# Two plain gate/up units instead of three at the edge into a feed-forward stage, with the third one's first two products as filler and a fixed order on three engines

## The chip, the core and the metric

The kernel runs on one core of one Trainium2 chip, in one launch. Times are device microseconds (us). The engines are TensorE (PE: matmuls and transposes, with its weight loads as PEld), VectorE (DVE), ScalarE (ACT), GpSimd (POOL) and SyncE (SP), which issues nearly all DMAs. Each engine takes its instructions in the order in which they stand in its own queue. Results of matmuls lie in PSUM, in eight banks; all else lies in SBUF.

## The reference

Two layers over a sequence of 512 tokens with 1024 channels. Layer 0 mixes tokens by stick-breaking attention, layer 1 by a gated MLP over chunks. Behind each mixer comes a SwiGLU feed-forward of width 2816, and this is where the change is:

```python
def swiglu(h, w_gate, w_up, w_down):
    return (jax.nn.silu(h @ w_gate) * (h @ w_up)) @ w_down

# at the end of a mixer, and ahead of the feed-forward behind it
x = x + gate * rms_norm(y, mix_post_g[i])
shift, scale, gate = ada_modulation(c, ffn_ada_w[i], ffn_ada_b[i])
h = rms_norm(x, ffn_pre_g[i]) * (1.0 + scale) + shift
y = swiglu(h, ffn_w_gate[i], ffn_w_up[i], ffn_w_down[i])
x = x + gate * rms_norm(y, ffn_post_g[i])
```

All is float32. The kernel multiplies in a shorter matmul type and makes up for it: each operand is split into a high part (ACT copies it to that type) and a low part (DVE subtracts the high part), and each product is three matmuls: high x high, high x low, low x high.

## The kernel before

The 512 tokens are four tiles of 128. `out_proj` (L545) ends a mixer: it accumulates the projection y of each tile in two PSUM banks, and hands each finished tile to `boundary` (L473). This makes, in order: the squares of y (ACT), their root, y times the gate G (DVE), the new residual x (DVE), its store (a POOL DMA), the squares of x and their root (ACT), the scaled and shifted t (DVE), eight transposes of t (PE) and the split of the transposed halves into hTh (ACT) and hTl (DVE). For tiles 0 and 1 it also keeps a float32 copy c (ACT). "Third tile" and "fourth tile" below are the tiles with tt of 2 and 3.

The feed-forward (`Ffn`, L1102) works on 22 pieces of 128 of its width. A plain unit (`unit`) makes gate and up of one piece for 256 tokens, as 2 x 8 x 3 matmuls of 256 columns; the first half takes tiles 0 and 1, the second half tiles 2 and 3. All other pieces go through `seven`, which makes gate and up for all 512 tokens together by seven products of half size, each 4 x 3 matmuls of 256 columns, instead of eight. For that it needs sums of the activations (`sums`: S1 to S4, from the kept copies c and the transposed third and fourth tile, split into Sh and Sl) and of the weights (`blocks`: x, b21, t13 and t24, each split; f13 and f24 are the float32 sums). A block's products stand in this order on PE: A11·B11 in bank R1, A12·B21 in R2, the previous block's A22·T4, then S1·T1 in a new bank R3, S2·T2 on top of R1, S4·B22 on top of R3, S3·T3 on top of R1. ACT copies R1 and R3 (tile e) before the next product is put on top. The generator `ahead` prepares the next block's weights in five steps between the products.

NH = 3: pieces 0, 1 and 2 are plain units, 3 to 21 are blocks. At the edge, `out_proj` takes the first halves of the three units (`first`, passed as `nxt`) one by one around the boundaries of the third and fourth tile; then come their second halves, then the blocks. Down to the second block the framework's scheduler decides where each engine's instructions stand. From there on (L1200) `pe["chain"]`, `dve.chain` and `act.chain` tie each instruction of the three engines to the one written before it.

Weights come by DMA on SP's queue, 512 KB each, into two `wraw` buffers (plain weights, and a block's x) and two `wraw2` buffers (a block's y). Their splits go to six pairs wh, wl. PSUM has six banks under tag b and two under tag p.

Of the kernel before, what the change touches and what calls it, by code (L numbers as in the profile page):

```python
# [8 lines left out]
F32 = mybir.dt.float32  # L9
F32R = mybir.dt.float32r  # L10
# [21 lines left out]
def trunk(ctx: ExitStack, tc: tile.TileContext, A: dict, out: bass.AP):  # L32
# [119 lines left out]
    def wemit():  # L152
# [4 lines left out]
        if src is None:  # L157
            for _ in blocks(*next_raws(n)):
                pass
            return  # L160
# [11 lines left out]
        else:  # L172
            act.activation(h[:], raw[:], AF.Copy)
            last_low[0] = nc.vector.tensor_tensor(l[:], raw[:], h[:].bitcast(F32), ALU.subtract)  # L174
# [31 lines left out]
    def blocks(xr, yr):  # L206

        fp = fwork["pool"]

        def high(t, src):  # L210
            act.activation(t[0][:], src, AF.Copy)

        def low(t, src):
            dve.tensor_tensor(t[1][:], src, t[0][:].bitcast(F32), ALU.subtract)

        def half(t, i):
            return lambda k: (t[0][:, 4 * i + k, :], t[1][:, 4 * i + k, :])

        x = wtile(KD, P)
        high(x, xr[:])  # L220
        f13 = fp.tile([P, KD, P], F32, tag="f13", name=nm("f13"))
        dve.tensor_tensor(
            f13[:].rearrange("p (a k) f -> p a (k f)", a=2),
            xr[:].rearrange("p (a k) f -> p a (k f)", a=2),
            yr[:, 4:8, :].rearrange("p (a k) f -> p a (k f)", a=1).to_broadcast([P, 2, 512]),
            ALU.add,
        )
        yield
        b21 = [fp.tile([P, 4, P], F32R, tag=f"b21{i}", name=nm("b21")) for i in range(2)]
        high(b21, yr[:, 0:4, :])  # L230
        t13 = wtile(KD, P)
        high(t13, f13[:])
        f24 = fp.tile([P, KD, P], F32, tag="f24", bufs=1, name=nm("f24"))
        dve.tensor_tensor(f24[:, 0:4, :], f13[:, 0:4, :], xr[:, 4:8, :], ALU.add)
        dve.tensor_tensor(f24[:, 4:8, :], f24[:, 0:4, :], yr[:, 0:4, :], ALU.add)
        yield
        low(x, xr[:])
        low(b21, yr[:, 0:4, :])
        yield
        t24 = wtile(KD, P)  # L240
        high(t24, f24[:])
        low(t13, f13[:])
        yield
        low(t24, f24[:])
        got.append({
            "B11": half(x, 0), "B22": half(x, 1), "B21": half(b21, 0),
            "T1": half(t13, 0), "T3": half(t13, 1), "T2": half(t24, 0), "T4": half(t24, 1),
        })

# [1381 lines left out]
```

## Time and profile before

| | us |
|---|---|
| median of 3 runs | 1125.38 |
| lowest, highest | 1118.23, 1127.74 |
| the profiled execution, its span | 1123.01, 1121.2 |
| edge of layer 0: first gate/up matmul, first matmul of a block | 276.6, 312.0 |
| edge of layer 1: first gate/up matmul | 772.2 |

The profile is of one execution. A row of the timeline gives start, length, engine, line in the kernel, operation, written tile <- read tiles and count; in brackets stands the idle time ahead of it and the instruction that ended it. Matmuls overlap: a row's length is that from its start to the modelled end of its result, and the distance to the next start is what it costs. An idle engine that nobody waits for costs nothing.

### The profile page before, as it was taken

How to read it: one execution, taken by the hardware profiler on the slowest of the kernel's cores; microseconds unless marked ns; L12 is line 12 of the kernel's file. 1: busy time of each engine (PE TensorE's matmuls, PEld its weight loads, DVE VectorE, ACT ScalarE, POOL GpSimd, SP SyncE). 2: the span in 40 equal slices, each digit the busy share in tenths (PEclk: the TensorE clock that was granted, in tenths of full speed). 3: DMA queues.
4: the chain of work that ended last, by engine and by line, in shares of the span. 5: the costliest groups of instructions: out<-in, count | busy, mean ns of one | idle time of the engine just before them, and what ended most of it. 6: DMA issues, size and time to landing. Idle time of an engine off the chain costs nothing.

```text
span 1121.2 us, 18515 instructions
## 1 busy us (share of the span) xinstructions
PE 1099.8 (98%) x7404; PEld 994.3 (89%) x7404; DVE 946.2 (84%) x1248; ACT 593.8 (53%) x982; POOL 29.6 (3%) x53
## 2 busy tenths in 40 slices
PE   6999999999999999999999999999999999999997
PEld 4787878788999999998888889988999999999995
DVE  4988999958989999879776867769979999899996
ACT  6454665656655555553253636437455555565652
POOL 0110100000000000000000000001000000000000
PEclk9999999999999999999999999999999999999999
DMA  8876434214424343359756375334224442332243
GB/s 335 331 246 208 148 91 131 91 59 155 161 78 167 132 162 121 114 208 345 251 192 243 132 269 164 101 125 150 96 95 151 149 147 89 106 113 95 76 142 122
DMA packets 51355, 176.38 MB, mean 157 GB/s; under 512 B 6074, under 2 KB 9146, under 8 KB 51268
## 3 DMA queue, kind: packets, MB, share of 16 engines
q1 hardware_dynamic: 48708, 166.81, 43.3%
q0 software_dynamic: 2560, 8.39, 2.1%
q8 instruction: 58, 0.95, 0.3%
q14 instruction: 29, 0.24, 0.1%
HBM read 164.69 MB, written 8.39 MB: 154 GB/s over the span
## 4 chain that ended last, share of the span: by engine, by line
PE 83%; DVE 9%; ACT 3%; DMA 3%; issue 2%; SPq 0%; DVEq 0%; ACTq 0%
PE r L107 33%; PE y L107 17%; PE v L107 8%; PE pqk L107 7%; PE u L107 4%; PE gu L107 4%; PE av L107 2%; PE z L107 2%; PE tw L115 1%; DVE wl L69 1%; DVE al L69 1%; DVE f L69 1%; DMA raw<-in_wdn 1%; DVE wl L174 1%; PE tp L115 1%
## 5 line engine op out<-in xcount | busy, mean ns | idle before, releaser
L85 ACT ACTIVATE wh<-raw 128x1024 fp32r<-128x1024 f32 (+1 forms) x112 | 115.7, 1037 | 134.5 <-PE y L107 44.1
L107 PE MATMUL r<-Sh,wl 128*128 128x256 f32 x608 | 170.2, 280 | 0.0
L107 PE MATMUL r<-Sh,wh 128*128 128x256 f32 x608 | 169.8, 279 | 0.0
L107 PE MATMUL r<-Sl,wh 128*128 128x256 f32 x608 | 169.6, 279 | 0.0
L107 PE MATMUL y<-wh,as 128*128 128x512 f32 x480 | 150.0, 390 | 0.0
L174 DVE TENSOR_TENSOR wl<-raw,wh 128x1024 fp32r<-128x1024 f32 x87 | 105.8, 1221 | 49.9 <-ACT wh L85 47.2
L107 PEld LDWEIGHTS r<-Sl,wh 128*128 128x128 f32 x608 | 114.3, 188 | 0.1
L107 PEld LDWEIGHTS r<-Sh,wl 128*128 128x128 f32 x608 | 114.1, 188 | 0.0
L107 PEld LDWEIGHTS r<-Sh,wh 128*128 128x128 f32 x608 | 113.7, 187 | 0.1
L107 PEld LDWEIGHTS y<-wh,as 128*128 128x128 f32 x480 | 90.0, 188 | 18.5
L69 DVE TENSOR_TENSOR wl<-f,wh 128x1024 fp32r<-128x1024 f32 x87 | 103.2, 1218 | 1.6 <-ACT wh L85 1.6
L85 ACT ACTIVATE e<-r 128x256 f32<-128x256 f32 x114 | 43.8, 384 | 109.8 <-PE r L107 106.1
L85 ACT ACTIVATE wh<-f 128x1024 fp32r<-128x1024 f32 x87 | 91.6, 1053 | 18.6 <-DVE f L69 11.9
L107 PE MATMUL y<-wl,as 128*128 128x512 f32 x240 | 93.7, 390 | 0.0
L107 PE MATMUL r<-hTh,wh 128*128 128x256 f32 x304 | 85.0, 280 | 0.1
L107 PE MATMUL r<-hTh,wl 128*128 128x256 f32 x304 | 85.1, 280 | 0.0
L107 PE MATMUL r<-hTl,wh 128*128 128x256 f32 x304 | 84.8, 279 | 0.0
L107 PE MATMUL r<-hTh,b 128*128 128x256 f32 x304 | 59.8, 279 | 0.0
L85 ACT ACTIVATE wh<-rawx 128x1024 fp32r<-128x1024 f32 x38 | 40.3, 1060 | 33.3 <-PE r L107 30.5
L107 PEld LDWEIGHTS r<-hTh,wh 128*128 128x128 f32 x304 | 56.9, 187 | 0.8 <-DVE gu L69 0.8
L107 PEld LDWEIGHTS r<-hTl,wh 128*128 128x128 f32 x304 | 57.1, 188 | 0.0
L107 PEld LDWEIGHTS r<-hTh,wl 128*128 128x128 f32 x304 | 57.1, 188 | 0.0
(260 smaller groups left out, 2936.1 us busy)
## 6 DMA issues: line engine op xcount, KB each, us to landing
rawada<-in_ada SPq DMA_DIRECT2D x80, 512.0 KB, 5.4
rawy<-in_wy SPq DMA_DIRECT2D x38, 512.0 KB, 4.3
rawx<-in_wx SPq DMA_DIRECT2D x38, 512.0 KB, 3.9
raw<-in_wdown SPq DMA_DIRECT2D x22, 512.0 KB, 5.5
raw<-in_wdn SPq DMA_DIRECT2D x22, 512.0 KB, 3.8
raw<-in_wqk SPq DMA_DIRECT2D x16, 512.0 KB, 4.2
ada<-in_ada0p SPq DMA_DIRECT2D x12, 512.0 KB, 7.8
raw<-in_wgu SPq DMA_DIRECT2D x12, 512.0 KB, 3.6
```

The costliest lines, as they stand in the source:

```text
L69: b = getattr(nc.vector, op)(*args, **kw)
L85: b = nc.scalar.activation(*args, **kw)
L107: b = nc.tensor.matmul(o, l, r, start=start, stop=stop, skip_group_check=True)
L115: last_tp[0] = nc.tensor.transpose(o, i, ident)
L174: last_low[0] = nc.vector.tensor_tensor(l[:], raw[:], h[:].bitcast(F32), ALU.subtract)
```

## The change

NH becomes 2, in both layers. Piece 2 becomes the first block, and its weights are laid out as x and y instead of gate and up. `out_proj` no longer calls the boundaries of the third and fourth tile itself: it hands them as two `Edge` objects to the new `Ffn.lead`, which has `boundary`'s steps as separate methods, sets the three chains at once, and writes the order out:

```diff
-    NH = 3
+    NH = 2
...
+        def lead(self, e2, e3):
+
+            pe["chain"] = dve.chain = act.chain = True
+            while len(raws) < taken[0] + 4:
+                wload()
+            e2.residual()
+            e2.scale()
+            e2.shift()
+            out = [self.unit(0, 0, 256)]
+            e3.residual()
+            self.ws[1] = [wget(("wgu", self.li, 1, 0), 0)]
+            e3.scale()
+            self.ws[1].append(wget(("wgu", self.li, 1, 1), 0))
+            e3.shift()
+            e2.turn()
+            e2.high()
+            out.append(self.unit(1, 0, 256, e3.turn))
+            b = Blocks(*next_raws(len(got)))
+            b.high("x")
+            b.low("x")
+            e2.low()
+            b.high("b21")
+            b.low("b21")
+            e3.high()
+            e3.low()
+            self.begun = self.seven(NH, None, None, True)
+            next(self.begun)
+            for f in out:
+                f()
+            sums(self.S, 2, e2.a)
+            b.sum13()
+            b.high("t13")
+            s3 = sum_parts(self.S, 3, e3.a)
+            next(s3)
+            self.unit(0, 256, 256)()
+            b.low("t13")
+            b.sum24()
+            b.high("t24")
+            b.low("t24")
+            for _ in s3:
+                pass
+            self.unit(1, 256, 256)()
...
             product(R1, "A11", "B11", True, False)
-            next(prep, None)
+            if not lead:
+                next(prep, None)
             act.activation(s1, R1, AF.Copy)
             product(R2, "A12", "B21", True, True)
-            next(prep, None)
+            if not lead:
+                next(prep, None)
             dve.tensor_tensor(gu[:, 0, lo], R2, s1, ALU.add)
+            if lead:
+                yield
             last = pending() if pending is not None else None
             next(prep, None)
+            R3 = bank("r3")[:, :256]
             product(R3, "1", "T1", True, False)
...
             next(prep, None)
             act.activation(s5, R3, AF.Copy)
             product(R1, "2", "T2", False, False)
```

`Edge` has the same instructions as `boundary`; `turn` are the eight transposes, `high` and `low` the split. `unit(1, 0, 256, e3.turn)` puts the fourth tile's transposes ahead of the unit's last twelve matmuls. `sum_parts` is `sums`, cut in two ahead of its fourth sum. `Blocks` has the steps of `blocks` as methods. The first block runs its first two products ahead of the two second halves, and the rest behind them; its preparation of the following block starts with the rest. Its tiles e and gu come from another pool. `units` takes up from the started block.

Three places show what this does to the queues. The first is DVE at the edge of layer 0, from the third tile's last steps on. t_402 is the third tile's t and t_425 the fourth's, wl_358 unit 0's low weights, wl_395 and wl_398 those of unit 1. Before:

```order
L69 TENSOR_TENSOR t_402_2663<-x_379_2484,A_145_676 128x1024
L174 TENSOR_TENSOR wl_358_2406<-raw_356_2403,wh_357_2405 128x1024
L174 TENSOR_TENSOR wl_395_2603<-raw_393_2600,wh_394_2602 128x1024
L69 RECIPROCAL r_409_2681<-sd_408_2679 128x1
L69 TENSOR_TENSOR t_425_2766<-y_326_2101,G_102_458 128x512
L69 SCALAR_TENSOR_TENSOR t_402_2663<-t_402_2663,r_409_2681,B_212_1198 128x1024
L69 TENSOR_SCALAR ss_426_2770<-sq_423_2764 128x1
L69 TENSOR_TENSOR t_425_2766<-y_327_2122,G_102_458 128x512
L69 RECIPROCAL r_428_2774<-sd_427_2772 128x1
L69 SCALAR_TENSOR_TENSOR x_392_2550<-t_425_2766,r_428_2774,x_392_2550 128x1024
L174 TENSOR_TENSOR wl_398_2609<-raw_396_2606,wh_397_2608 128x1024
```

And now, where t_397 and t_408 are the two tiles, wl_414 and wl_419 the low weights of unit 1 (unit 0's stand ahead of the third tile's residual):

```order
L69 SCALAR_TENSOR_TENSOR t_397_2606<-t_397_2606,r_404_2624,B_212_1198 128x1024
L69 TENSOR_TENSOR t_408_2679<-y_326_2101,G_102_458 128x512
L69 TENSOR_SCALAR ss_409_2683<-sq_406_2677 128x1
L69 TENSOR_TENSOR t_408_2679<-y_327_2122,G_102_458 128x512
L69 RECIPROCAL r_411_2687<-sd_410_2685 128x1
L69 SCALAR_TENSOR_TENSOR x_392_2550<-t_408_2679,r_411_2687,x_392_2550 128x1024
L69 TENSOR_TENSOR wl_414_2694<-raw_393_2600,wh_413_2693 128x1024
L69 TENSOR_TENSOR t_408_2679<-x_392_2550,A_145_676 128x1024
L69 TENSOR_TENSOR wl_419_2704<-raw_394_2602,wh_418_2703 128x1024
L69 RECIPROCAL r_417_2701<-sd_416_2699 128x1
L69 SCALAR_TENSOR_TENSOR t_408_2679<-t_408_2679,r_417_2701,B_212_1198 128x1024
```

Unit 1's first low weights moved from ahead of the third tile's shift to behind the fourth tile's residual, and the two tiles no longer mix.

The second place is DVE ahead of the first block's third product in layer 0. There fs are the fourth tile's sums, Sl their low parts, wl_456 the low part of t13, wl_463 that of t24, f13_470 the sum of the block after. Now:

```order
L69 TENSOR_TENSOR Sl_449_2848<-fs_458_2871,Sh_448_2847 128x4x128
L69 TENSOR_TENSOR Sl_447_2846<-fs_457_2870,Sh_446_2845 128x4x128
L69 TENSOR_TENSOR act_441_2836<-silu_460_2928,gu_459_2879 128x256
L69 TENSOR_TENSOR wl_456_2868<-f13_454_2865,wh_455_2867 128x1024
L69 TENSOR_TENSOR f24_461_2932<-f13_454_2865,rawx_429_2784 128x512
L69 TENSOR_TENSOR f24_461_2932<-f24_461_2932,rawy_430_2785 128x512
L69 TENSOR_TENSOR wl_463_2936<-f24_461_2932,wh_462_2935 128x1024
L69 TENSOR_TENSOR fs_458_2871<-fs_457_2870,c_378_2482 128x512
L69 TENSOR_TENSOR Sl_451_2850<-fs_458_2871,Sh_450_2849 128x4x128
L69 TENSOR_TENSOR Sl_445_2844<-fs_457_2870,Sh_444_2843 128x4x128
L69 TENSOR_TENSOR act_441_2836<-silu_465_2993,gu_464_2944 128x256
L69 TENSOR_TENSOR f13_470_3003<-rawx_431_2788,rawy_432_2789 128x1024
```

Before, the same sums stood between the steps of two blocks (wl_445 and wl_448 are the low parts of t13 and t24 of the first block, f24_458 and wl_452 belong to the second):

```order
L69 TENSOR_TENSOR wl_445_2819<-f13_441_2813,wh_444_2818 128x1024
L69 TENSOR_TENSOR Sl_468_2917<-fs_475_2924,Sh_467_2916 128x4x128
L69 SCALAR_TENSOR_TENSOR fs_477_2938<-fs_477_2938,tp_434_2795 128x512
L69 TENSOR_TENSOR wl_448_2827<-f24_446_2821,wh_447_2826 128x1024
L69 TENSOR_TENSOR fs_478_2939<-fs_477_2938,c_374_2471 128x512
L69 TENSOR_TENSOR f24_458_2846<-f13_453_2838,rawx_437_2806 128x512
L69 TENSOR_TENSOR Sl_470_2919<-fs_477_2938,Sh_469_2918 128x4x128
L69 TENSOR_TENSOR f24_458_2846<-f24_458_2846,rawy_438_2807 128x512
L69 TENSOR_TENSOR wl_452_2836<-rawx_437_2806,wh_451_2835 128x1024
```

The block's own weights moved from ahead of the fourth tile's sums to between and behind them, and the second block's weights moved behind all of them.

The third place is ACT in layer 0, from the fourth tile's last sums to the copies of the first block. e_439<-r3_471 is the copy of R3, wh_468, b21_472 and wh_474 are the next block's x, b21 and t13. Now:

```order
L85 ACTIVATE wh_462_2935<-f24_461_2932 128x1024
L85 ACTIVATE Sh_450_2849<-fs_458_2871 128x4x128
L85 ACTIVATE Sh_444_2843<-fs_457_2870 128x4x128
L85 ACTIVATE silu_465_2993<-gu_464_2944 128x256
L85 ACTIVATE wh_468_3000<-rawx_431_2788 128x1024
L85 ACTIVATE b21_472_3018<-rawy_432_2789 128x512
L85 ACTIVATE wh_474_3021<-f13_470_3003 128x1024
L85 ACTIVATE e_439_2808<-r3_471_3005 128x256
L85 ACTIVATE e_439_2808<-r1_437_2806 128x256
L85 ACTIVATE wh_477_3069<-f24_476_3024 128x1024
```

Before, with the copies into e_488 and the next free block's weights in wh_497:

```order
L85 ACTIVATE wh_459_2851<-f24_458_2846 128x1024
L85 ACTIVATE silu_484_3105<-gu_483_3056 128x256
L85 ACTIVATE e_488_3111<-r1_485_3108 128x256
L85 ACTIVATE e_488_3111<-r3_487_3110 128x256
L85 ACTIVATE e_488_3111<-r1_485_3108 128x256
L85 ACTIVATE wh_497_3212<-rawx_449_2831 128x1024
L85 ACTIVATE e_493_3194<-r1_490_3191 128x256
```

Three high parts of the following block now stand between the last sums and the copy of R3, where before the first block's three copies followed one another.

More of the change, by code (lines that the diff above doesn't have):

```diff
@@ L157, in wemit @@
         if src is None:
-            for _ in blocks(*next_raws(n)):
+            for _ in Blocks(*next_raws(n)).steps():
                 pass
@@ L173, in wemit @@
             act.activation(h[:], raw[:], AF.Copy)
[L174 removed]
+            low = dve if act.chain else nc.vector
+            last_low[0] = low.tensor_tensor(l[:], raw[:], h[:].bitcast(F32), ALU.subtract)
         got.append((h, l))
@@ L204, in next_raws @@
         return raws[n]
[L206 to L248, printed above, removed]
@@ L254, in ahead @@
             if stream[n][0] is None:
-                yield from blocks(*next_raws(n))
+                yield from Blocks(*next_raws(n)).steps()
             else:
```

157 lines of the change are left out of this document (134 added, 23 removed).

## The prediction, made before the run

> **What bounds the kernel now.** I read the busy table first, then the chain of waits, then TensorE's timeline with its idle times at the two edges that the change rewrites, then busy time by stretch.
>
> ```profile
> PE 1099.8 (98%) x7404; PEld 994.3 (89%) x7404; DVE 946.2 (84%) x1248; ACT 593.8 (53%) x982; POOL 29.6 (3%) x53
> ```
>
> TensorE (PE) is busy 98% of the span. From the chain of waits, start and length in us:
>
> ```profile
> 291.09 21.09 PE gu L107 x186
> 312.18 173.73 PE r L107 x1476
> ```
>
> After the first edge the chain stays on PE without a break: 1476 matmuls in 173.73 us, 0.1177 us each. That is the price of one 256-column matmul below. PE's timeline, with the idle time ahead of an instruction in brackets, has one wait at each edge, for the fourth tile's transposes:
>
> ```profile
> 290.00 1.09 PE L115 MATMUL tp<-identt,t 128*128 128x128 f32 x8 [0.31 <-DVE t L69]
> ...
> 786.35 1.09 PE L115 MATMUL tp<-identt,t 128*128 128x128 f32 x8 [1.11 <-DVE t L69]
> ```
>
> So 1.4 us of waiting is there to be won, and no more. Busy time by stretch (columns: stretch, length, then busy us of PE, PEld, DVE, ACT, POOL):
>
> ```profile
> 276.00:291.00 15.00, 14.69 (x123) 14.37 (x122) 14.67 (x19) 11.46 (x21) 2.03 (x3) 1.00 0.61 211
> 291.00:312.00 21.00, 21.00 (x187) 21.00 (x187) 20.58 (x30) 11.49 (x18) 0.00 (x0) 1.00 0.40 126
> 312.00:330.00 18.00, 18.00 (x156) 18.00 (x155) 12.98 (x20) 9.00 (x16) 0.00 (x0) 1.00 0.28 88
> 330.00:400.00 70.00, 70.00 (x596) 70.00 (x596) 63.95 (x83) 37.25 (x64) 0.00 (x0) 1.00 0.41 144
> ```
>
> VectorE (DVE) is busy 35.25 of the edge's 36 us. PE hides that only because six stretches of 48 plain matmuls lie beside it and DVE's order fills every gap. Behind the edge DVE works 91% of the time, so a backlog that it takes along melts by only 0.9 us in a block of ten.
>
> **Part by part: what goes.** A plain unit is 96 matmuls, a seven-product block 84; per layer one unit becomes a block, so 24 matmuls go: 24 x 0.1177 = 2.8 us, all on PE's path. The two waits above go too: 1.4 us.
>
> **What comes: DVE work under less cover.** The filler lets the first block start before its sums exist, but between the first gate/up matmul and the block's third product only 48 + 48 + 24 + 96 = 216 matmuls lie, where 288 and the block's first two products lay: 96 fewer, 11.3 us less cover, while DVE has an additional block to prepare and its order is now a chain. The trace of before doesn't show the new order, so I lay it out instruction by instruction from these rows of DVE and of ScalarE (ACT), layer 0 first.
>
> ```profile
> 273.13 1.29 DVE L69 TENSOR_TENSOR hTl<-tp,hTh 128x512 fp32r<-128x512 f32 x2
> 274.53 1.28 DVE L69 SCALAR_TENSOR_TENSOR x<-t,r,x 128x1024 f32<-128x1024 f32 x1
> 275.85 1.23 DVE L69 TENSOR_TENSOR t<-x,A 128x1024 f32<-128x1024 f32 x1
> ...
> 289.86 1.22 DVE L174 TENSOR_TENSOR wl<-raw,wh 128x1024 fp32r<-128x1024 f32 x1
> 291.00 1.22 DVE L69 TENSOR_TENSOR f<-rawx,rawy 128x1024 f32<-128x1024 f32 x1
> ...
> 293.93 0.41 DVE L69 TENSOR_TENSOR act<-silu,gu 128x256 f32<-128x256 f32 x1
> 294.26 0.68 DVE L69 TENSOR_TENSOR f<-f,rawy 128x512 f32<-128x512 f32 x1
> ...
> 296.93 0.68 DVE L69 SCALAR_TENSOR_TENSOR fs<-fs,tp 128x512 f32<-128x512 f32 x1
> 297.64 1.29 DVE L69 TENSOR_TENSOR fs<-fs,c 128x512 f32<-128x512 f32 x2
> ```
>
> From one start to the next: 1.14 us for 1024 columns, 0.60 for 512 (0.71 where it needs the one before it), 0.33 for 256.
>
> ```profile
> 273.86 1.20 ACT L85 ACTIVATE c<-tp 128x512 f32<-128x512 f32 x2
> 274.95 2.00 ACT L85 ACTIVATE wh<-raw 128x1024 fp32r<-128x1024 f32 x2
> 276.84 1.05 ACT L85 ACTIVATE junk<-x 128x1024 bf16<-128x1024 f32 x1
> 277.79 0.19 ACT L85 ACTIVATION_READ_ACCUMULATOR junk<-x 128x1 f32 x1
> 278.01 0.29 ACT L85 ACTIVATE sd<-sx,epsb 128x1 f32<-128x1 f32 x1
> ...
> 298.37 0.63 ACT L85 ACTIVATE Sh<-fs 128x512 fp32r<-128x512 f32 x1 [2.08 <-DVE fs L69]
> ...
> 317.76 0.38 ACT L85 ACTIVATE e<-r 128x256 f32<-128x256 f32 x1 [1.08 <-PE r L107]
> ...
> 768.51 1.20 ACT L85 ACTIVATE c<-tp 128x512 f32<-128x512 f32 x2
> ```
>
> PE starts unit 0 here, in layer 0 and in layer 1:
>
> ```profile
> 276.64 0.28 PE L107 MATMUL gu<-hTh,wh 128*128 128x256 f32 x1
> ...
> 772.18 0.28 PE L107 MATMUL gu<-hTh,wh 128*128 128x256 f32 x1
> ```
>
> Third tile: unit 0's low weights now stand ahead of the third tile's residual on DVE (in before, most of that residual ran first), and their high part starts on ACT when the copies to c end, about 275.0. High 1.0, low 1.14: DVE is free at 277.2. Residual (0.66, 0.6, a reciprocal, 1.28) ends at 280.1, square, accumulator and root on ACT at 281.6, reciprocal and shift at 283.0. PE is through 48 matmuls at 276.64 + 5.65 = 282.3: it waits 0.7 us for the turn, which takes 1.09.
>
> Unit 1's weights: their high part stands on ACT behind the fourth tile's root, their low part on DVE behind its whole residual. High: about 284.2 to 285.3. Residual ends at 285.8, low part at 287.0. PE arrives at 284.1 and the third matmul takes the low weights, at 287.0 instead of 284.4: 2.6 us. All of PE is queued behind that.
>
> Filler: the block's x comes into the buffer that unit 1's low part gives back at 287.0:
>
> ```profile
> rawx<-in_wx SPq DMA_DIRECT2D x38, 512.0 KB, 3.9
> ```
>
> Landed at 291, high 292.1, low 293.3, about when PE arrives (293.5, after 48 matmuls and the turn): 0.1, bounded by 0 and 1.5 for a landing of 3.9 to 5.4 us. The second product's b21 low stands behind two lows of the third tile: 0.4. Unit 0's second half takes a PSUM bank that the sum of the two products gives back: 0.6. Together 1.1.
>
> Sums: PE runs the two second halves, 96 matmuls, from 297.5 to 308.8. DVE from 297.1: three of 256 columns to 298.1; the third tile's sums (2.1, wait 0.66 for ACT's high part, lows 1.2, fourth sum 0.7, wait 0.66, lows 1.2) to 304.6; f13 to 305.8; the fourth tile's first half (2.1 + 0.66 + 1.2) to 309.8; a product to 310.1; T1/T3 low to 311.3. PE's third product therefore waits 0.5 for the sums' low part and 1.9 for T1's: 2.4. f24 to 312.7, its high part on ACT to 313.8, low to 315.0: the product with T2 waits 1.3 and 1.0: 2.3; it ends at 316.3.
>
> The copy behind the next block: the product with B22 overwrites R3, so it needs ACT's copy s5 of R3. In the chained order that copy stands behind the high part of the next block's t13, which needs the next block's f13, which DVE reaches after the fourth tile's last sums: 315.0 + 0.7 + 0.66 + 1.2 + 0.33 = 317.9, f13 to 319.1, high 1.0, copy 0.38: 320.5. PE waits 320.5 - 316.3 = 4.2 us. After that I find no wait above 0.2: the next block's x low (321.7) is there when PE comes to it (323.3).
>
> Layer 0: 0.7 + 2.6 + 1.1 + 2.4 + 2.3 + 4.2 = 13.3. In layer 1 unit 0's low weights stand further ahead: the residual waits only for a square behind the copies to c, which end at 769.7, and starts at 770.3, 1.9 us before unit 0 instead of 0.6 after it. The turn then waits for nothing, unit 1's weights 0.5, the filler 0.7; the last three are the same: 10.1. Sum: 23.4 - 2.8 - 1.4 = +19.2. Not counted: two loads more of y and x, two fewer of gate/up, on the same SP queue, all of 512 KB, each waiting for its buffer as before.
>
> The profiled execution took 1123.0 us (span 1121.2): 1142.2; from the median, 1125.4, it would be 1144.6. I say 1143.
>
> [...] A wait of 4.2 us is longer than any that PE has here between its first matmul and its last. What an idle PE does to its clock shows at the span's end (the eighth figure is the granted clock), and at its start:
>
> ```profile
> 1110.00:1115.00 5.00, 3.83 (x17) 2.82 (x16) 3.54 (x7) 1.43 (x4) 0.00 (x0) 1.00 0.46 157
> 1115.00:1121.20 6.20, 0.00 (x0) 0.00 (x0) 2.18 (x4) 0.61 (x3) 0.00 (x0) 0.69 0.36 127
> ...
> 7.65 3.92 PE L115 MATMUL tp<-identt,x 128*128 128x128 f32 x16 [7.65 <-DVE x L69]
> ```
>
> PE stops at 1113.8 and the clock falls some time after 1115. Sixteen transposes after 7.65 us of idleness took 3.92 us where two turns of eight take 2.18: at most 1.74 us lost, some of it waiting for data. [...] If the clock falls to half, a mean of 0.69 over 6.2 us puts the fall at 1117.4, 3.5 us after PE's last work. [...]
>
> **Rivals.**
> 1. *DVE is in time.* Place: the third product of the first block, at 308.8. If DVE gets from the gu sum to T1's low part in 11.3 us instead of 14.2, and the next block's f13 in time, the 8.9 us of each layer fall away and 4.4 + 1.2 of early waits stay: 1123.0 - 4.2 + 5.6 = 1124, not slower. For it: in before DVE ran 20.58 of 21 us. Against: that was by interleaving independent steps, which the chain forbids; each half of the sums now waits twice for ACT.
> 2. *The copy gets through.* Decides: whether PE finishes the T2 product after the next f13 rather than before. Then the last 4.2 us of each layer go: 1142.2 - 8.4 = 1133.8. For it: every earlier wait that grows shortens this one. Against: both stand on the same DVE list.
> 3. *The backlog stays.* If the next two blocks also wait, 1.5 us each: 4 x 1.5 more, 1148. For it: 91% busy. Against: x low comes 1.6 us early.
> 4. *The clock falls* in the 4.2 us waits, 1.74 us each as bounded above: 1145.7.
>
> **How the numbers follow.** Forecast 0.60; rival 1 0.08, rival 2 0.12, rival 3 0.12, rival 4 0.08. The forecast's own bounds are the landing of x (0 to 1.5 per layer) and the gaps between dependent DVE steps (0 to 0.11 over some twenty of them per layer): 1138 to 1145 from the profiled execution, up to 1148 from the median. The range of 1132 to 1150 takes in rivals 2 to 4 and leaves out rival 1 and the ends. A measurement here can tell about 1% from no change. 1% above the median is 1136.6: slower 0.78 (forecast nearly whole, rivals 3 and 4), within 1% 0.20 (rivals 1 and 2), faster 0.02.
>
> **What would show it.** In the new profile: PE waits at both edges for low weights (gu <- DVE wl), for T1 and T2 (r <- DVE wl, ACT wh), and about 4 us for ACT e; from the first gu matmul of layer 0 to that of layer 1 507 us instead of 495.5; no wait within the later blocks. Wrong: PE without a gap across the edge, an e copy that runs ahead of the next block's wh, or later blocks longer than 9.9 us.

## The result and the profile after

| | before | after |
|---|---|---|
| median, us | 1124.55 (6 runs) | 1145.35 (6 runs) |
| lowest, highest of those in the ratio | 1118.23, 1127.85 | 1135.01, 1147.99 |
| the profiled execution, its span | 1123.01, 1121.2 | 1142.70, 1140.8 |

The ratio is 1.0139, 95% interval 1.0100 to 1.0177: slower by 1.4%, with the lower end at the 1% that can be told here. Two of the six executions after took 3849 us, for a reason that no profile shows, and are left out of the ratio, but not of the median; the other four have a median of 1140.7.

The same views as before. TensorE (PE) is busy 97% of the span, 98% before:

```profile
PE 1102.3 (97%) x7380; PEld 993.9 (87%) x7380; DVE 958.0 (84%) x1262; ACT 597.8 (52%) x992; POOL 29.5 (3%) x53
```

24 matmuls fewer, and 2.5 us more busy time. In PE's timeline, where each edge had one wait, there are now nine and six:

```profile
283.88 1.06 PE L115 MATMUL tp<-identt,t 128*128 128x128 f32 x8 [0.64 <-DVE t L69]
285.78 0.39 PE L107 MATMUL gu<-hTh,wh 128*128 128x256 f32 x1 [0.84 <-ACT wh L85]
287.57 0.39 PE L107 MATMUL gu<-hTh,wl 128*128 128x256 f32 x1 [1.29 <-DVE wl L69]
299.07 0.38 PE L107 MATMUL gu<-hTh,wh 128*128 128x256 f32 x1 [0.59 <-DVE gu L69]
311.23 0.38 PE L107 MATMUL r<-Sl,wh 128*128 128x256 f32 x1 [0.34 <-DVE Sl L69]
313.29 0.39 PE L107 MATMUL r<-Sh,wl 128*128 128x256 f32 x1 [1.68 <-DVE wl L69]
315.71 0.39 PE L107 MATMUL r<-Sh,wh 128*128 128x256 f32 x1 [0.97 <-ACT wh L85]
316.97 0.39 PE L107 MATMUL r<-Sh,wl 128*128 128x256 f32 x1 [0.76 <-DVE wl L69]
322.39 0.58 PE L107 MATMUL r<-Sh,wh 128*128 128x256 f32 x1 [3.97 <-ACT e L85]
...
790.17 0.39 PE L107 MATMUL gu<-hTh,wl 128*128 128x256 f32 x1 [0.81 <-DVE wl L69]
800.53 0.39 PE L107 MATMUL gu<-hTh,wh 128*128 128x256 f32 x1 [0.58 <-DVE gu L69]
812.39 0.39 PE L107 MATMUL r<-Sl,wh 128*128 128x256 f32 x1 [0.16 <-DVE Sl L69]
814.46 0.58 PE L107 MATMUL r<-Sh,wl 128*128 128x256 f32 x1 [1.68 <-DVE wl L69]
818.14 0.40 PE L107 MATMUL r<-Sh,wl 128*128 128x256 f32 x1 [0.46 <-DVE wl L69]
823.56 0.58 PE L107 MATMUL r<-Sh,wh 128*128 128x256 f32 x1 [3.96 <-ACT e L85]
```

From top to bottom these are the third tile's turn, unit 1's weights (two rows), the bank that the filler's sum gives back, the low sums, T1, T2 (two rows) and the copy; in layer 1 unit 1's weights, the bank, the low sums, T1, T2 and the copy. They add up to 11.1 and 7.7 us. VectorE's (DVE's) timeline has the reason in the same place: it stands idle for 0.70 us behind each of ScalarE's (ACT's) high parts of the sums, and for 1.12 behind that of t24:

```profile
302.72 1.29 DVE L69 TENSOR_TENSOR Sl<-fs,Sh 128x512 fp32r<-128x512 f32 x2 [0.70 <-ACT Sh L85]
305.31 1.29 DVE L69 TENSOR_TENSOR Sl<-fs,Sh 128x512 fp32r<-128x512 f32 x2 [0.70 <-ACT Sh L85]
310.48 1.29 DVE L69 TENSOR_TENSOR Sl<-fs,Sh 128x512 fp32r<-128x512 f32 x2 [0.70 <-ACT Sh L85]
315.69 1.22 DVE L69 TENSOR_TENSOR wl<-f,wh 128x1024 fp32r<-128x1024 f32 x1 [1.12 <-ACT wh L85]
```

The three rows with a length of 0.58 behind a wait, where the others have 0.38 to 0.40, show something else: after some of the waits PE runs at half its clock. Busy time by stretch (length, then busy us of PE, PEld, DVE, ACT, POOL, and the granted clock):

```profile
285.42:288.83 3.41, 1.76 (x12) 1.56 (x13) 3.23 (x3) 2.69 (x6) 1.49 (x2) 1.00 0.28 113
288.83:292.25 3.42, 3.42 (x18) 3.42 (x17) 2.58 (x3) 1.48 (x4) 0.00 (x0) 0.50 0.92 258
312.72:316.14 3.42, 1.87 (x12) 1.54 (x12) 2.26 (x4) 1.06 (x1) 0.00 (x0) 1.00 0.33 86
316.14:319.55 3.41, 1.52 (x11) 1.25 (x10) 2.71 (x5) 2.00 (x4) 0.00 (x0) 1.00 0.56 223
319.55:322.96 3.41, 0.57 (x2) 0.57 (x3) 3.34 (x5) 2.84 (x6) 0.00 (x0) 0.50 0.00 0
322.96:326.38 3.42, 3.42 (x18) 3.42 (x17) 1.63 (x3) 1.65 (x2) 0.00 (x0) 0.50 0.51 147
```

The clock is 0.50 in whole steps of 3.41 us here: one from 288.83, two from 319.55, and in layer 1 one from 814.48 and two from 821.31. A matmul of 256 columns starts 0.213 us after the one ahead of it there, instead of 0.118. Over both layers that is 5.6 us: 1.6 and 1.8 behind the two copies, 1.5 behind unit 1's weights in layer 0, and the rest at T1 in layer 1. This is no accident of the profiled execution: the mean granted clock is 0.985 to 0.990 in all four of this kernel that are in the ratio, and 0.996 to 0.999 in all those of before that have it on record.

And a third thing works the other way. Behind the edge, in 140 us in which PE never waits, the two layers do not do the same number of matmuls:

```profile
340.00:480.00 140.00, 140.00 (x1238) 140.00 (x1237) 131.90 (x173) 78.97 (x134) 0.00 (x0) 1.00 0.41 144
840.00:980.00 140.00, 140.00 (x1191) 140.00 (x1190) 127.76 (x166) 76.44 (x130) 0.00 (x0) 1.00 0.40 140
```

Layer 0 goes at 0.1131 us a matmul, layer 1 at 0.1175, with the clock at 1.00 in both. In the profile of before both layers have 1191 here:

```profile
340.00:480.00 140.00, 140.00 (x1191) 140.00 (x1191) 125.78 (x164) 75.01 (x127) 0.00 (x0) 1.00 0.38 134
840.00:980.00 140.00, 140.00 (x1191) 140.00 (x1190) 126.15 (x165) 76.28 (x130) 0.00 (x0) 1.00 0.37 129
```

Start by start in after's timeline there are two paces, 0.1133 and 0.1178, and nothing between; layer 0 of this execution caught the faster one behind 334 us and kept it for 1427 matmuls, which saved 6.4 us. Which layer has which pace does not go with the change: in the experiments below it is layer 0, layer 1, both or neither. So I compare kernels by a length that a pace cannot blur: from the first gate/up matmul to the first matmul of the down projection behind the last r matmul in layer 0, and to the end of the last r matmul that reads the sums in layer 1, plus 0.0045 us for each matmul that ran at the faster pace. The rest of the span is left out: over all profiled executions here it is 270.3 to 270.9 us between the two stages, 123.7 to 124.8 behind them, and 276 to 281 ahead of the first, which alone moves a total by up to 5 us. Before has 225.2 + 224.3 + 1.0 (221 fast ones) = 450.5 us, after 234.7 + 234.7 + 6.4 = 475.8. **At one pace the change costs 25.3 us, 5.6 of them by the clock.**

### The profile page after: what moved, and what is told of

The parts are those of the page before. It is cut to its first block, busy times and chain, and to the rows that moved or that the text cites. A ratio compares the mean times of both kernels' runs of the same rounds, so it can differ in the third digit from the quotient of the medians.

```text
span 1140.8 us, 18482 instructions
## 1 busy us (share of the span) xinstructions
PE 1102.3 (97%) x7380; PEld 993.9 (87%) x7380; DVE 958.0 (84%) x1262; ACT 597.8 (52%) x992; POOL 29.5 (3%) x53
## 4 chain that ended last, share of the span: by engine, by line
PE 84%; DVE 8%; ACT 4%; DMA 2%; issue 1%; SPq 0%; DVEq 0%; ACTq 0%
PE r L107 34%; PE y L107 17%; PE pqk L107 6%; PE v L107 5%; PE X L107 4%; PE u L107 4%; PE Y L107 3%; PE av L107 2%; PE z L107 2%; PE tw L115 1%; PE Z L107 1%; PE W L107 1%; PE tp L115 1%; PE ab L107 1%; DVE fs L69 1%
## 5 line engine op out<-in xcount | busy, mean ns | idle before, releaser
L107 PE MATMUL r<-Sh,wh 128*128 128x256 f32 x640 | 181.3, 283 | 8.9 <-ACT e L85 7.9
L107 PE MATMUL r<-Sh,wl 128*128 128x256 f32 x640 | 180.7, 282 | 4.6 <-DVE wl L69 4.6
L107 PE MATMUL r<-Sl,wh 128*128 128x256 f32 x640 | 180.5, 282 | 0.5 <-DVE Sl L69 0.5
L85 ACT ACTIVATE wh<-raw 128x1024 fp32r<-128x1024 f32 (+1 forms) x108 | 111.4, 1035 | 129.0 <-PE y L107 42.0
L175 DVE TENSOR_TENSOR wl<-raw,wh 128x1024 fp32r<-128x1024 f32 x77 | 93.8, 1220 | 48.4 <-ACT wh L85 47.9
L107 PEld LDWEIGHTS r<-Sh,wh 128*128 128x128 f32 x640 | 122.6, 192 | 9.9 <-ACT e L85 8.3
L107 PEld LDWEIGHTS r<-Sh,wl 128*128 128x128 f32 x640 | 122.7, 192 | 5.5 <-DVE wl L69 5.5
L107 PEld LDWEIGHTS r<-Sl,wh 128*128 128x128 f32 x640 | 122.4, 191 | 1.0 <-DVE Sl L69 0.9
L69 DVE TENSOR_TENSOR wl<-f,wh 128x1024 fp32r<-128x1024 f32 x91 | 107.7, 1218 | 2.9 <-ACT wh L85 2.9
L85 ACT ACTIVATE wh<-f 128x1024 fp32r<-128x1024 f32 x91 | 95.9, 1054 | 26.7 <-DVE f L69 26.5
```

The lines of the kernel that those rows point to most:

```text
L69: b = getattr(nc.vector, op)(*args, **kw)
L85: b = nc.scalar.activation(*args, **kw)
L107: b = nc.tensor.matmul(o, l, r, start=start, stop=stop, skip_group_check=True)
L175: last_low[0] = low.tensor_tensor(l[:], raw[:], h[:].bitcast(F32), ALU.subtract)
```

## The experiments

All edits are to the changed kernel unless said otherwise. "Waits" is the sum of the brackets at the two edges, "half" what half-clock matmuls took beyond 0.118 each, "two stages" the length just defined, from each run's profiled execution.

| | median, us | ratio to before, 95% | waits | half | two stages |
|---|---|---|---|---|---|
| before | 1124.55 | | 1.4 | 0 | 450.5 |
| after | 1145.35 | 1.0100 to 1.0177 | 18.7 | 5.6 | 475.8 |
| 1 scheduler's order | 1125.62 | 0.9963 to 1.0049 | 2.6 | 0 | 450.5 |
| 2 two units, old edge | 1136.16 | 1.0081 to 1.0156 | 9.8 | 1.9 | 461.0 |
| 3 copy first | 1144.64 | 1.0144 to 1.0227 | 12.4 | 5.3 | 470.4 |
| 4 spare products | 1145.94 | 1.0148 to 1.0239 | 11.1 | 3.9 | 471.4 |
| 5 VectorE's order free | 1135.90 | 1.0064 to 1.0119 | 9.3 | 5.2 | 463.0 |
| 6 ScalarE's order free | 1152.70 | 1.0193 to 1.0264 | 17.6 | 7.9 | 477.3 |
| 7 scheduler's order, lows last | 1124.44 | 0.9970 to 1.0005 | 0.7 | 0 | 449.0 |
| 8 spare matmuls for the pace | 1129.60 (1 run) | | 0.7 | 0 | 453.3 |
| 9 written order from the filler on | 1140.92 | 1.0107 to 1.0210 | 14.0 | 5.4 | 470.1 |
| 10 written order from T1 on | 1130.68 | 1.0018 to 1.0076 | 9.2 | 3.8 | 461.0 |
| 11 copy's wait filled | 1131.46 | 1.0057 to 1.0116 | 1.0 | 0 | 456.4 |
| 12 copy first, from T1 on | 1129.93 | 1.0033 to 1.0090 | 6.0 | 0 | 454.6 |

### 1. The scheduler's order at the edge

```diff
 def lead(self, e2, e3):
-    pe["chain"] = dve.chain = act.chain = True
...
 def units(self, bg0):
+    pe["chain"] = dve.chain = act.chain = True
     rest = next(self.begun)
```

> Same work as the changed kernel (two units, the filler, the same steps); only the fixed order of the three engines begins behind the edge instead of ahead of it, so the scheduler places the edge's steps. Theory (the order written out makes DVE wait at each of its dependent steps while steps that need nothing stand behind): DVE's idle gaps of 0.7 to 1.5 us between 290 and 318 close, TensorE's waits at the two edges fall from 18.7 us to under 4, the clock stays at 1.00, and the time is 1120 to 1130. Rival (two units give 96 matmuls less cover, whatever the order): DVE is still late at the block's third product by the 11.3 us less cover that it has, minus what the filler gives back (2.8), so 1134 or more.

The time is that of before, and the two stages are too. PE's timeline of layer 0 and the chain of waits behind it:

```profile
291.17 0.38 PE L107 MATMUL r<-hTh,wh 128*128 128x256 f32 x1 [0.26 <-ACT wh L85]
295.79 0.38 PE L107 MATMUL gu<-hTl,wh 128*128 128x256 f32 x1 [0.31 <-DVE hTl L69]
308.31 0.38 PE L107 MATMUL r<-Sl,wh 128*128 128x256 f32 x1 [0.75 <-DVE Sl L69]
```

```profile
308.31 181.18 PE r L107 x1535
```

DVE has one gap of note left between 279 and 309 us, of 0.40. The first block's f13 and the first half of its f24 (the two rows of f) stand where it waited for ACT's root:

```profile
287.38 1.22 DVE L69 TENSOR_TENSOR f<-rawx,rawy 128x1024 f32<-128x1024 f32 x1
288.63 0.69 DVE L69 TENSOR_TENSOR f<-f,rawx 128x512 f32<-128x512 f32 x1
289.72 0.16 DVE L69 RECIPROCAL r<-sd 128x1 f32<-128x1 f32 x1 [0.40 <-ACT sd L85]
```

PE takes three matmuls of the filler ahead of the fourth tile's transposes. 181.18 / 1535 = 0.1180, the slower pace. The instructions are the same as in the changed kernel, but for four more loads of ACT's function table (996 instructions of ACT's, 992 in after; 1.28 us each), so the written order costs the 25.3 us. Two units with the filler cost nothing by themselves, and win nothing: the 2.8 us of fewer matmuls do not show.

### 2. Two units at the old edge

Before, with NH = 2 and the weights laid out for it; no filler, no `lead`.

```diff
-    NH = 3
+    NH = 2
...
-            evacs.append(nxt[2]())
+            evacs.extend(f() for f in nxt[2:])
```

> The kernel before with two units instead of three and nothing else: no filler, no fixed order ahead of the second block. Theory (cover counts too, but the order is the larger part): the block's first product and the fourth tile's transposes come 48 matmuls (5.6 us) earlier, so TensorE waits 4 to 6 us for the fourth tile's scaled rows in each layer, the clock falls behind that, and the time is 1130 to 1138. Rival (all of the loss is the fixed order): no wait over 1.2 us, time 1119 to 1126.

As expected by the theory. The lost cover turns up mainly in one wait of each layer, for the fourth tile:

```profile
298.02 1.97 PE L115 MATMUL tp<-identt,t 128*128 128x128 f32 x8 [5.37 <-DVE t L69]
...
799.08 1.97 PE L115 MATMUL tp<-identt,t 128*128 128x128 f32 x8 [4.09 <-DVE t L69]
```

With experiment 1 this gives the worth of `lead` in the scheduler's order: 461.0 - 450.5 = 10.5 us over both layers, 1.9 of them by the clock. That the filler makes up all of it is not shown, since `lead` also puts the fourth tile's transposes in another place.

### 3 and 4. The copy's wait: the copy first, and the wait filled

```diff
+            if lead:
+                act.activation(s5, R3, AF.Copy)
             next(prep, None)
-            act.activation(s5, R3, AF.Copy)
+            if not lead:
+                act.activation(s5, R3, AF.Copy)
```

> The changed kernel, but in the first block ScalarE copies R3 before the next block's second preparation step instead of after it. Theory (the copy is late because the next block's sums stand ahead of it, but VectorE's backlog stands behind both): the wait for e goes from 4.0 us to about 2, since the fourth sum's parts, which the same product needs, come no earlier than now; 0.5 to 1 us comes back as waits for the next block's operands; time 1137 to 1141. Rival (the copy alone is the price): 4.0 us and the half clock behind it go in each layer, 1131 to 1134. Rival (nothing is won, the product waits as long for something else): 1141 to 1145.

```diff
+            if lead:
+                for _ in range(2):
+                    product(R2, "A12", "B21", True, True)
             product(R3, "4", "B22", False, True)
```

> The changed kernel with 24 more matmuls in each layer, the second product twice more into its own bank when nothing reads it any longer, in the wait of 4.0 us ahead of the product with B22. They take 24 x 0.1177 = 2.8 us of a wait that lasts 4.0. Theory of the clock (a stretch in which TensorE idles long enough halves its clock for one or two steps of 3.41 us): the matmuls behind the wait run at 0.118 us each instead of 0.213, which gives back 1.8 us in layer 0 and 2.0 in layer 1: time 1137 to 1140 for a kernel that does more work, against 1142.7. Rival (the clock has nothing to do with this wait): the pace of 0.213 stays, time 1142 to 1144. Rival (the wait is not idle for TensorE): 5.6 us more, 1148.

Both medians miss what the theories said: 1144.64 lies where the rival without any gain had it, and 1145.94 between the ranges of the two rivals. Yet the waits did what was expected in the first, the two stages are 5.4 us shorter, and the bracket for e fell further than I said, to 0.8, because PE came later: it ran T2's product at half clock. In the second the spare products take up the copy's wait, yet 3.9 of the 5.6 us of the clock stay: it had already fallen at T1 and T2, in a step in which PE idled for 1.95 us (308.93 to 312.35 there), well ahead of the copy. So my theory had the place of it wrong. The totals could not have told either: the runs of these two reach from 1137 to 1150 us, and both profiled executions caught the faster pace in one layer. Experiments 11 and 12 ask this again where the copy is nearly the only wait.

### 5 and 6. One engine's order free

The first has VectorE's chain set behind the edge, the second ScalarE's; the other two stay set.

```diff
-    pe["chain"] = dve.chain = act.chain = True
+    pe["chain"] = act.chain = True
```

The second edit frees more than ScalarE. The kernel ties VectorE's low parts of the plain units' weights only where ScalarE's chain is set, so these left VectorE's written order too:

```python
            low = dve if act.chain else nc.vector
```

> The changed kernel, with only VectorE's order at the edge left to the scheduler; TensorE's and ScalarE's stay written out until the edge is over. Theory (VectorE's list, with its gaps behind each ScalarE step, is the larger part): its waits at T1 and T2 shrink (5.5 us of those in layer 0, 3 in layer 1), the sums are ready with the third product, and of the copy's 4.0 us about 1 goes, since ScalarE still makes the next block's high parts ahead of it; the weights' 2.1 us in layer 0 stay, because ScalarE's list holds the high part. Waits of 8 to 10 us in all, and time 1128 to 1136. Rival (all three orders together): no change, 1140 to 1147.

> The changed kernel, with only ScalarE's order at the edge left to the scheduler. Theory (VectorE's list bounds): unit 1's high weights may come earlier, but VectorE's low parts keep their places, so the waits at T1, T2 and the copy stay as they are, 4 us for the copy; time 1140 to 1148, as the changed kernel. Rival (the copy waits because of ScalarE's own list): the 4.0 us go in each layer and the time is 1131 to 1136.

The first came as its theory had it. VectorE's list is half of the matter: 12.8 us of the 25.3 go with it, and the waits at T1 and T2 are gone. Those for unit 1's weights stay, and of the copy's 4.0 us 2.6 stay in each layer; ACT's and PE's lists are still the written ones. Its profiled execution caught the faster pace in both layers (1238 matmuls in 140 us twice), so that it took 1125.08 where the median is 1135.90: a reading from one execution would have called this kernel as fast as before.

The second's median, 1152.70, lies above both ranges. The waits for unit 1's weights are gone and the copy waits 2.91 instead of 3.97, but there are new losses that neither theory had. In layer 0 it is mainly the third tile's turn:

```profile
287.10 1.06 PE L115 MATMUL tp<-identt,t 128*128 128x128 f32 x8 [2.35 <-DVE t L69]
```

It waits 2.35, where after has 0.64. On DVE one of the freed low parts now stands ahead of this tile's shift and waits for its high part there:

```profile
284.33 1.23 DVE L175 TENSOR_TENSOR wl<-raw,wh 128x1024 fp32r<-128x1024 f32 x1 [1.14 <-ACT wh L85]
285.67 1.28 DVE L69 SCALAR_TENSOR_TENSOR t<-t,r,B 128x1024 f32<-128x1024 f32 x1
```

In layer 1 the fourth tile's turn waits 1.50 and in after not at all: ACT now makes unit 0's SiLU ahead of that tile's root, with a table load of 1.28 us before each of the two. Since the edit freed low parts of VectorE's as well, what ScalarE's order is worth alone stays open.

### 7. The scheduler's order, with the lows last

Experiment 1 with the copy first as in 3, and the first block's product with T1 in another order of its twelve matmuls:

```diff
+            def lows_last(o, a, b, start):
+                for u, v in ((0, 0), (0, 1), (1, 0)):
+                    for k in range(4):
+                        mm(o, W[b](k)[v], S[a](k)[u], start and u == v == k == 0, False)
...
+            if lead:
+                lows_last(R3, "1", "T1", True)
+            else:
                 product(R3, "1", "T1", True, False)
```

> The free order, with two further edits in the first block alone: ScalarE copies R3 ahead of the next block's second preparation step, and the product with T1 takes its eight matmuls with high rows first and its four with low rows last. Theory: the waits that the free order left there (0.75 and 0.47 for the low sums, 0.64 for the copy) go, and what remains at the two edges is under 1.5 us, so that it takes the 24 fewer matmuls, 2.8 us, and most of before's waits of 1.4: 1119 to 1126, 1 to 3 us under the kernel before, which the total alone can hardly tell. Rival (another operand is late in their place): 1124 to 1130.

Of the waits, 0.31 and 0.35 are left, one in each layer. The two stages are 1.5 us shorter than before's; the median is 1.2 us under before's in the same session (1125.63), and the interval still holds no change. This is all that two units are worth here.

### 8. What sets the pace

```diff
             if not lead:
+                n = 12 * (f - NH) - 4 * self.li
+                mm(R[:, 256 : 256 + n], W["B21"](0)[0], S["A12"](0)[0][:, :n], True, True)
                 next(prep, None)
```

> The kernel of the run before it with one spare matmul in each of the 19 later blocks of a layer, into columns of a bank that nothing reads: 12, 24, ... 228 columns wide in layer 0, and 8, 20, ... 224 in layer 1; it is there to see TensorE's pace, which is 0.1178 us per 256-column matmul in most stretches of these traces and 0.1133 in some, and changes at stalls of a few hundredths of a microsecond. Theory (two stable positions of weight load and matmul to each other, which a shift can flip): the pace changes between blocks at some of the widths, and stays until a later one flips it back; time then 1113 to 1124. Rival (the pace is set by something else in a run, as the place of its buffers): one pace through all blocks of a layer, and the time is that of the run before plus the spare matmuls, 2 to 4 us.

The theory fell: through all 38 spare matmuls the pace stays 0.1178. This is the rival's one pace; the time, of a single execution, is 5.2 us above experiment 7's median, where 2 to 4 were expected. The 140 us that held 1191 or 1238 matmuls of a block hold, with the spare ones among them:

```profile
340.00:480.00 140.00, 140.00 (x1191) 140.00 (x1191) 126.10 (x164) 74.95 (x128) 0.00 (x0) 1.00 0.39 136
840.00:980.00 140.00, 140.00 (x1192) 140.00 (x1191) 126.08 (x164) 75.05 (x127) 0.00 (x0) 1.00 0.38 136
```

In its parent, experiment 7, layer 1 had the faster pace (1238). Where the other timelines show the pace change, a weight load had just been held up, be it by some 20 ns (in after the load at 334.07 starts 0.14 us behind the one ahead, where the others have 0.12), or the clock had just come back to full (831.6 in experiment 3); not every hold-up changes it (835.51 in after, of the same size). This kernel's later blocks have no such hold-up.

### 9 and 10. Where in the written order

The chains are set later in `lead`: in the first ahead of `b = Blocks(...)`, in the second ahead of `b.low("t13")`.

> The changed kernel with the written order beginning at the first block's preparation: the last two tiles' residuals, scales, shifts and turns and unit 1's weights are the scheduler's to place, and all that follows (filler, sums, T1, T2, copy) is in the written order as before. Theory (the later waits are made by the order of the sums, not handed down from the earlier ones): the waits of 0.64, 0.84, 1.29 and 0.81 for the third tile and unit 1's weights go, 3.6 us, and those at T1 (1.7), T2 (about 1.5) and the copy (4.0) stay in both layers, so 14 to 15 us of waits; time 1137 to 1144. Rival (the later waits are the earlier ones' backlog): all shrink, 1128 to 1134.

> The changed kernel with the written order beginning only at the low part of T1, behind the sums of both tiles' first halves. Theory: the waits at the third product go; of T2 under 1 us is left; the copy's 4.0 us stay in both layers with the half clock behind them, since what stands ahead of the copy (the fourth tile's last sums, the next block's sum and high part) is still in the written order: 8 to 10 us of waits, time 1130 to 1137. Rival (the copy is late only because VectorE is late): the copy's wait shrinks as well, to under 2 us, 1124 to 1128.

Both medians lie in the theory's range, and the waits are 14.0 and 9.2 us, as expected; only the copy waits 2.92 in the first, and not 4.0. The later waits are not handed down from the earlier ones: with the residuals and unit 1's weights in the scheduler's places T1 still waits 1.68 in both layers, and with the sums in its places as well the copy still waits as long as in after:

```profile
314.71 0.58 PE L107 MATMUL r<-Sh,wh 128*128 128x256 f32 x1 [3.98 <-ACT e L85]
315.09 0.41 PE L107 MATMUL r<-Sl,wh 128*128 128x256 f32 x1
315.30 0.41 PE L107 MATMUL r<-Sh,wl 128*128 128x256 f32 x1
```

So the 25.3 us, with the clock's share in them, divide by place: 475.8 - 470.1 = 5.7 for the two tiles and unit 1's weights, 9.1 from the filler to the sums, 461.0 - 450.5 = 10.5 for T2 and the copy.

### 11 and 12. The copy by itself

Both start from experiment 10: the first with three spare products ahead of the product with B22, the second with the copy first.

> The kernel of the run before (order written out only from T1's low part on) with 36 spare matmuls in each layer's copy wait, the second product three times more into its own bank: 36 x 0.1177 = 4.24 us, as long as the wait from the end of one matmul to the start of the next. No operand comes earlier, so without an effect of the clock the time is unchanged, 1130.7. Theory of the clock (it halves for a step of 3.41 us after a step in which TensorE idled for 1.65 us or more, and did not after 1.54 or less): no such step is left, no matmul runs at 0.213, and the 20 half-rate matmuls of each layer give back 20 x 0.095 = 1.9 us: 1126 to 1129, with 72 matmuls more. Rival (the half rate comes from the stall, not from idleness, and follows any long dependence on another engine): pace 0.213 stays, 1130 to 1132.

> The same kernel (order written out only from T1's low part on, no spare matmuls) with ScalarE's copy of R3 ahead of the next block's second preparation step. Theory (the fourth tile's last sum, which the same product reads, stands on the same VectorE list): of the 4.0 us about 2 stay, for the high part of that sum, as in the first run with this edit, where they turned to 0.8 behind the slowed product; about 1 us turns up at the next operands; with 2 us less waiting per layer the clock may stay whole: 1125 to 1129. Rival (copy alone): all 4.0 go, 1120 to 1124.

In the first no matmul runs at half clock, with 72 matmuls more and each of them in what was idle time. The row behind the filled wait starts 0.12 us after the last spare one:

```profile
315.63 0.28 PE L107 MATMUL r<-hTh,b 128*128 128x256 f32 x1
315.75 0.28 PE L107 MATMUL r<-Sh,wh 128*128 128x256 f32 x1
315.87 0.28 PE L107 MATMUL r<-Sl,wh 128*128 128x256 f32 x1
```

The two stages are 4.6 us shorter than experiment 10's, of which 3.8 were its half clock. So at this place it was idleness that made the clock fall, and not the long dependence of the rival. The granted clock of every execution bears this out: 0.992 to 0.994 in the ten of experiment 10, 0.997 to 0.999 in the eight of this one. That filling a wait pays in the total is not shown: the median, 1131.46, lies in the rival's range, and the ratio to before is 1.0086 against experiment 10's 1.0047. Experiment 10's ten runs reach from 1127.0 to 1135.8, and only the profiled execution's pace is known.

In the second 1.83 of the copy's 4.0 stay, and 0.52, 0.35 and 0.47 come back at the next operands, as expected in size, but for another reason than I gave. PE's row, and ACT's timeline ahead of the copy (the row of e):

```profile
314.20 0.38 PE L107 MATMUL r<-Sh,wh 128*128 128x256 f32 x1 [1.83 <-ACT e L85]
311.51 1.15 ACT L85 ACTIVATE Sh<-fs 128x512 fp32r<-128x512 f32 x2 [1.89 <-DVE fs L69]
312.57 0.36 ACT L85 ACTIVATE silu<-gu 128x256 f32<-128x256 f32 x1
312.83 1.05 ACT L85 ACTIVATE wh<-rawx 128x1024 fp32r<-128x1024 f32 x1
313.78 0.37 ACT L85 ACTIVATE e<-r 128x256 f32<-128x256 f32 x1
```

It is the copy itself that PE waits for, behind three steps: the fourth tile's last high parts, which waited for DVE's sum, unit 1's SiLU and the next block's x. The clock stays whole at both edges, and the two stages are 6.4 us shorter than in 10. The median, 1129.93, lies just over the expected range.

## Why the prediction was right, and where it was not

It said 1143, 1132 to 1150, slower with 0.78. The median is 1145.35 of six executions and 1140.7 of the four in the ratio, and the order of events is the one that was laid out. From the first gate/up matmul of layer 0 to that of layer 1 it took 505.0 us, where 507 was given as a sign, and the waits have the operands that were named. Term by term, predicted and as bracketed in the profile:

| | layer 0 | layer 1 |
|---|---|---|
| third tile's turn | 0.7 / 0.64 | 0 / 0 |
| unit 1's weights | 2.6 / 2.13 | 0.5 / 0.81 |
| filler | 1.1 / 0.59 | 0.7 / 0.58 |
| T1 and the low sums | 2.4 / 2.02 | 2.4 / 1.84 |
| T2 | 2.3 / 1.73 | 2.3 / 0.46 |
| the copy | 4.2 / 3.97 | 4.2 / 3.96 |

**The terms were near, the sum left two things out.** 23.4 was forecast and 18.7 is in the brackets; two terms are well off, the filler (the loaded x and b21's low part came in time, only the bank waited) and layer 1's T2, which its half-clock product ahead of it hid. A bracket is also less than what a wait costs: at 313.29 the start is 2.06 us behind the one before it, 1.94 more than the pace, for a bracket of 1.68, and the next matmul comes after 0.23 instead of 0.118. Summed in this way over the fifteen waits, the restarts come to some 4.6 us. Then the clock took 5.6, and the pace gave 6.4 back where before had 1.0 of it. From before's two stages, 225.2 + 224.3: 449.5 - 2.8 - 1.4 + 18.7 + 5.6 - 6.4 + 1.0 = 464.2. Measured are 469.4, so 5.2 are left, most of them the restarts. That the forecast of +19.2 met +19.6 in the profiled execution is partly luck: what it overstated (4.7 of waits) and what the faster pace gave (5.4) came to about as much as what it left out (5.6 and 5.2). At one pace the change cost 25.3.

**Rival 4, the clock, came, and leaving it out of the sum was the step that was wrong.** It was given 0.08 because the waits of 4.2 us only just pass 3.5, an estimate from the span's end in before's profile. There PE's last matmul ends at 1113.8, and the granted clock is 1.00 from 1116 to 1117 and 0.50 from 1118 to 1119. Behind the two copies the clock cost 1.6 and 1.8 us, where rival 4 had 1.74 each; that bound came from the sixteen transposes at the span's start, where the profile shows no clock under 1.00. In after the falls at 288.83, 319.55 and 814.48 lie 30.72 and 494.93 us apart, 9 and 145 times 3.413. What stood ahead of a fall was not always one long wait: at 288.83 the clock fell behind waits of 0.84 and 1.29 with matmuls between them, in a step whose PE was idle for 1.65 of 3.41 us. This place and T1 in layer 1, which rival 4 did not name, make the loss 5.6 us instead of 3.5.

**Rival 1, DVE in time,** is false for the written order and true for the scheduler's (experiment 1: 450.5, before's own figure). "By interleaving independent steps, which the chain forbids" is the sentence that the experiments bear out; experiment 5 shows that DVE's list is half of it. Of the rest, ACT's place for the copy is a part: moving it alone shortens the two stages by 5.4 us (experiment 3). What PE's list adds was not tried alone.

**Rival 2, the copy gets through,** did not come: in experiment 10, with no wait left at T1 and 0.73 or less at T2, the copy still waits 3.98. What it waits for stands on both lists, as rival 2's "against" had it: moved ahead of one step of ACT's, it keeps 1.83 (experiment 12). **Rival 3, a backlog that stays,** did not come either: PE is busy 140.00 of 140 us behind both edges, and after the copy's row there is no bracket in the later blocks.

**The smaller cover** was given as 96 matmuls, 11.3 us in each layer, and went into the sum only through the waits. Two units without the filler cost 10.5 us over both layers (experiment 2), and with it, in the scheduler's order, nothing (experiment 1). That part of the change did what it was written for; the prediction did not part it from the written order.

## What to carry to other kernels

An order written out by hand costs what it keeps apart: before fixing a queue, look for each step that waits for another engine and put there something that needs neither, as the scheduler did here with f13 and f24. Freeing one engine's list at a time, and setting the fixed order later and later, tells in a few runs whose list it is and where, as long as each edit frees only the list that it names. And ask how much of a stretch PE stands idle, not only how long one wait is: at the two edges here the clock fell behind every step of 3.41 us with 1.87 us idle or more and behind none with 1.54 or less, and two waits of 0.84 and 1.29 us cost it in after, where one of 1.83 in experiment 12 did not.

## What the runs showed that was not expected

**The clock fell on a share, not on a gap.** In all profiles here, at the two edges, no step of 3.41 us at full clock in which PE idled for 1.54 us or less was followed by half clock (thirteen steps with 0.91 to 1.54), every one with 1.87 or more was, and of those between 1.65 and 1.84 six were and two were not. These two are in experiment 12 (idle is the length less PE's 1.63 and, in layer 1, 1.68), where the step behind one stays at 1.00:

```profile
312.63:316.05 3.42, 1.63 (x12) 1.43 (x12) 3.35 (x6) 3.12 (x7) 0.00 (x0) 1.00 0.02 6
316.05:319.46 3.41, 3.11 (x27) 3.11 (x28) 3.41 (x6) 2.28 (x4) 0.00 (x0) 1.00 0.25 59
```

What decides in between stays open. A step that was itself at half clock was followed by another when PE idled for 0.50 us or more in it (24 steps), and by full clock when it idled for 0.22 or less (20 steps). Where a step begins matters: the waits of 0.64, 0.84 and 1.29 in layer 0 come as 0.63, 0.84 and 1.28 in experiment 4, where the steps part them into 1.47 and 1.28 us of idle time and no half clock follows; in after 1.65 falls into one step, and it does.

**Two paces.** In these profiles, with a weight load to every matmul (7380 of each in after), a stream of 256-column matmuls ran at 0.1133 or at 0.1178 us each, 4% apart, with the clock at 1.00, and kept its pace for 1427 matmuls in after (334.1 to 496.3) and some 1660 in before (787.4 to 983.3). It changed where a weight load was held up (by some 20 ns at 334.07 in after) or the clock came back (831.6 in experiment 3); 38 spare matmuls of 8 to 228 columns did not change it, and what sets it stays open. A whole layer at the faster pace is 6.4 to 6.7 us less: it was in one layer of after and of experiments 3, 4 and 7, in both of experiment 5, and in no whole layer of the others. That before's runs reach from 1116.5 to 1128.7 over the sessions fits one layer and two at the faster pace, but only profiled executions show a pace, so this was not shown.
